# Row-wise cosine similarity on one core: hardware loops per engine with aligned heads, other pieces of the last two blocks, and stores awaited behind a manual section

## The chip, the cores and the metric

One core of a Trainium2 chip runs the whole program. The time is device microseconds (us) of one execution. The kernel before takes 1251.18 us (median of 4 runs in the comparison, 1250.94 to 1251.31). The profile is one execution recorded by the hardware profiler. Its span, from the first to the last instruction, is about 1.8 us shorter than the time of the same run.

## The reference

```python
x, y: 8192 x 8192, float32
x_norm = np.linalg.norm(x, axis=1, keepdims=True)
y_norm = np.linalg.norm(y, axis=1, keepdims=True)
return np.sum(x * y, axis=1) / (x_norm.squeeze() * y_norm.squeeze() + 1e-8)
```

Every element is read once: 536.87 MB. ACT squares and sums x and y, and DVE forms the dot product.

## The kernel before

The first 60 row blocks of 128 rows come in 30 groups of two blocks. Each group is one 8 MB load of x and one of y, so 60 loads go into three slots. The last four blocks are loaded in pieces that get smaller towards the end, so that little is left to compute when the last byte lands. A framework makes the waits between instructions. It unrolls everything: there is no branch between the first load and the end.

```python
PIECES = {
    nt - 4: [("x", 8192, "A"), ("y", 8192, "A")],
    nt - 3: [("x", 8192, "A"), ("y", 8192, "A")],
    nt - 2: [("x", 8192, "A"), ("y", 4096, "A"), ("y", 4096, "A")],
    nt - 1: [("x", 4096, "A"), ("y", 3072, "A"), ("x", 2432, "A"), ("y", 1792, "A"),
             ("y", 1408, "A"), ("x", 1024, "A"), ("y", 640, "A"), ("y", 640, "A"),
             ("x", 640, "V"), ("y", 256, "A"), ("y", 384, "A")],
}   # "A": ACT squares this piece, "V": DVE does
# ... cut: the slots, the sums, the first load ...
for g in range(G):                                     # G = 30, unrolled
    xt, yt = xs.pop(g), ys.pop(g)
    c = 2 * g
    cut = 2 * K - SIDE
    square(xt[:, 0:K], col(XX, c))                     # ACT
    square(xt[:, K:], col(XX, c + 1))
    # ... cut ...
    nc.vector.tensor_copy(out=side, in_=xt[:, cut:])   # DVE
    dot(xt[:, 0:K], yt[:, 0:K], col(XY, c), xt[:, 0:K])
    dot(xt[:, K:cut], yt[:, K:cut], part, xt[:, K:cut])
    square(yt[:, 0:K], col(YY, c))
    square(yt[:, K:], col(YY, c + 1))
    dot(side, yt[:, cut:], col(XY, c + 1), side, part)
    if g + 1 < G:
        load(g + 1)
# ... cut: for each piece of the last blocks a square and, for y, a dot ...
    if b == last - 1:
        finish(nt - NB, last)      # square root and reciprocal of the finished blocks
# ... cut: the last chain: base <- sums of the parts; last dot; transposes; product; store ...
```

Of the kernel before, what the change touches and what calls it, by code (L numbers as in the profile page):

```python
# [7 lines left out]


FP32 = mybir.dt.float32  # L10
U8 = mybir.dt.uint8
ALU = mybir.AluOpType
ACTF = mybir.ActivationFunctionType
AX = mybir.AxisListType
EPS = 1e-8
XX, YY, XY = 0, 1, 2


def lead_with_first_load(nc):


    blocks = nc.m.functions[0].blocks
    opening, body = blocks[0], blocks[1]
    load = next(i for i in body.instructions if i.opcode == "DMACopy")
    assert not load.sync_info.on_wait
    rest = [i for i in body.instructions if i.name != load.name]
    head = list(opening.instructions)
    at = next(n for n, i in enumerate(head) if i.opcode == "Drain" and i.engine == load.engine)
    head.insert(at, load)
    body.instructions = rest  # L30
    opening.instructions = head
# [3 lines left out]
def kernel(  # L35
# [6 lines left out]
    nc = tc.nc  # L42
    P = nc.NUM_PARTITIONS
    nc.at_finalize(lead_with_first_load)
    n_rows, K = x.shape
    nt = n_rows // P

# [3 lines left out]
    NB = 4  # L51
    G = (nt - NB) // 2
    SIDE = 4096
    BANK = 512
    VJUNK = 3072

    xg = x[0:G * 2 * P, :].rearrange("(g p j) k -> g p (j k)", p=P, j=2)
    yg = y[0:G * 2 * P, :].rearrange("(g p j) k -> g p (j k)", p=P, j=2)
# [4 lines left out]
    PIECES = {  # L63
        nt - 4: [("x", 8192, "A"), ("y", 8192, "A")],
        nt - 3: [("x", 8192, "A"), ("y", 8192, "A")],
        nt - 2: [("x", 8192, "A"), ("y", 4096, "A"), ("y", 4096, "A")],
        nt - 1: [("x", 4096, "A"), ("y", 3072, "A"), ("x", 2432, "A"), ("y", 1792, "A"),
                 ("y", 1408, "A"), ("x", 1024, "A"), ("y", 640, "A"), ("y", 640, "A"),
                 ("x", 640, "V"), ("y", 256, "A"), ("y", 384, "A")],
    }  # L70

    slots = ctx.enter_context(tc.tile_pool(name="slots", bufs=3))
    junkpool = ctx.enter_context(tc.tile_pool(name="junk", bufs=1))
    small = ctx.enter_context(tc.tile_pool(name="small", bufs=1))
    psumpool = ctx.enter_context(
        tc.tile_pool(name="psum", bufs=1, space=bass.MemoryType.PSUM))

    def slot(name):
        return slots.tile([P, 2 * K], FP32, tag="slot", name=name)

    xs, ys = {}, {}

    def load(g):
        xs[g] = slot(f"xg{g}")
        nc.sync.dma_start(out=xs[g], in_=xg[g])
        ys[g] = slot(f"yg{g}")
        nc.sync.dma_start(out=ys[g], in_=yg[g])

    def load_block(b):
        s = slot(f"b{b}")  # L90
        xs[b], ys[b] = s[:, 0:K], s[:, K:]
        at = {"x": 0, "y": 0}
        for which, w, _ in PIECES[b]:
            a = at[which]
            at[which] = a + w
            dst, src = (xs[b], xv) if which == "x" else (ys[b], yv)
            nc.sync.dma_start(out=dst[:, a:a + w], in_=src[b, :, a:a + w])

    load(0)

    sums = small.tile([P, 3, nt], FP32, tag="sums")
    norm = small.tile([P, 2, nt], FP32, tag="norm")
    den = small.tile([P, nt], FP32, tag="den")
    ident = small.tile([P, P], FP32, tag="ident")
    dummy = small.tile([P, 1], FP32, tag="dummy")
    junk = junkpool.tile([P, K], U8, tag="junk")
    vjunk = junkpool.tile([P, VJUNK], U8, tag="vjunk")

    nc.scalar.memzero(dummy)  # L109
    nc.scalar.sqrt(out=dummy, in_=dummy)  # L110
    make_identity(nc, ident)

    def square(src, acc, into=junk):
        nc.scalar.activation(out=into, in_=src, func=ACTF.Square, accum_out=acc)  # L114

    def dot(a, b, acc, into, init=0.0):
        nc.vector.tensor_tensor_reduce(  # L117
            out=into, in0=a, in1=b, scale=1.0, scalar=init, op0=ALU.mult, op1=ALU.add,
            accum_out=acc)

    def col(q, c):
        return sums[:, q, c:c + 1]
# [3 lines left out]
    for g in range(G):  # L126
        xt, yt = xs.pop(g), ys.pop(g)
        c = 2 * g
        cut = 2 * K - SIDE
        square(xt[:, 0:K], col(XX, c))  # L130
        square(xt[:, K:], col(XX, c + 1))
        side = psumpool.tile([P, SIDE], FP32, tag="side", name=f"side{g}")
        part = small.tile([P, 1], FP32, tag="part", name=f"part{g}")
        nc.vector.tensor_copy(out=side, in_=xt[:, cut:])  # L134
        dot(xt[:, 0:K], yt[:, 0:K], col(XY, c), xt[:, 0:K])
        dot(xt[:, K:cut], yt[:, K:cut], part, xt[:, K:cut])
        square(yt[:, 0:K], col(YY, c))
        square(yt[:, K:], col(YY, c + 1))
        dot(side, yt[:, cut:], col(XY, c + 1), side, part)
        if g + 1 < G:  # L140
            load(g + 1)

    for b in PIECES:
        load_block(b)

    def finish(a, b):

        c = slice(a, b)
        nc.scalar.activation(out=norm[:, :, c], in_=sums[:, 0:2, c], func=ACTF.Sqrt)  # L149
        nc.vector.tensor_mul(out=den[:, c], in0=norm[:, 0, c], in1=norm[:, 1, c])  # L150
        nc.vector.tensor_scalar_add(out=den[:, c], in0=den[:, c], scalar1=EPS)
        nc.vector.reciprocal(out=den[:, c], in_=den[:, c])  # L152

    def store_groups(ps):
        c = slice(0, 2 * G)
        res = small.tile([P, 2 * G], FP32, tag="res")
        nc.vector.tensor_mul(out=res, in0=sums[:, XY, c], in1=den[:, c])  # L157
        orow = small.tile([G, P, 2], FP32, tag="orow")
        for j in range(2):
            nc.tensor.transpose(out=ps[j], in_=res[:, j:2 * G:2], identity=ident)  # L160
            nc.vector.tensor_copy(out=orow[:, :, j], in_=ps[j])  # L161
        nc.sync.dma_start(
            out=out[0:G * 2 * P].rearrange("(g q) -> g q", q=2 * P),
            in_=orow.rearrange("g p j -> g (p j)"))


    tail = psumpool.tile([P, SIDE], FP32, tag="side", name="tail")
    pst = [tail[0:G, j * BANK:j * BANK + P] for j in range(2)]
    psl = [tail[0:NB, j * BANK:j * BANK + P] for j in range(2, 4)]


    ring = {"A": 0, "V": 0}

    def room(engine, w):
        tile_, size = (junk, K) if engine == "A" else (vjunk, VJUNK)
        a = ring[engine] if ring[engine] + w <= size else 0
        ring[engine] = a + w
        return tile_[:, a:a + w]

    last = nt - 1  # L180
    for b, pieces in PIECES.items():
        nx = sum(1 for q in pieces if q[0] == "x")
        ny = len(pieces) - nx
        parts = sums[:, :, b:b + 1]
        if ny > 1:
            m = max(nx, ny - 1 if b == last else ny)
            parts = small.tile([P, 3, m], FP32, tag=f"parts{b}", name=f"parts{b}")
            nc.vector.memzero(parts)
        if b == last:
            base = small.tile([P, 3], FP32, tag="base")  # L190
            fin = small.tile([P, 1], FP32, tag="fin")
        at, k = {"x": 0, "y": 0}, {"x": 0, "y": 0}
        for n, (which, w, engine) in enumerate(pieces):
            a, i = at[which], k[which]
            at[which], k[which] = a + w, i + 1
            src = (xs if which == "x" else ys)[b][:, a:a + w]
            if b < last or n < len(pieces) - 1:
                acc = parts[:, XX if which == "x" else YY, i:i + 1]
                xy, init = parts[:, XY, i:i + 1], 0.0
            else:  # L200
                nc.vector.tensor_reduce(out=base, in_=parts, axis=AX.X, op=ALU.add)  # L201
                acc, xy, init = fin, col(XY, last), base[:, XY:XY + 1]
            if engine == "A":
                square(src, acc, room("A", w))
            else:
                dot(src, src, acc, room("V", w))
            if which == "y":
                xp = xs[b][:, a:a + w]
                dot(xp, src, xy, room("V", w) if w <= VJUNK else xp, init)
        if ny > 1 and b != last:  # L210
            nc.vector.tensor_reduce(  # L211
                out=sums[:, :, b:b + 1], in_=parts, axis=AX.X, op=ALU.add)
        if b == nt - 4:
            finish(0, 2 * G)
            store_groups(pst)
        if b == last - 1:
            finish(nt - NB, last)

# [44 lines left out]
```

## Time and profile before

| | kernel before |
|---|---|
| time, median | 1251.18 us |
| first slot landed (ACT's first square starts at 21.98) | 21.95 us |
| 60th slot landed | 1165.48 us |
| last input landed | 1244.08 us |
| last dot starts | 1245.58 us |
| last store's receipt (the signal that it is complete) | 1248.63 us |
| span | 1249.46 us |

Landings are read from the semaphore increments of each load, of which the sixteenth counts (the trace of before has 1269 increments: 16 for each of the 78 loads and the first store, 5 for the last store); the small tables of this document use them. The profile's page gives the overview. Its DMA row shows the busy share of the DMA engines in tenths over 40 equal slices, and the next row the rate. The section of queues shows packets, megabytes and the share of time.

```profile
span 1249.5 us, 876 instructions
...
PE 1.3 (0%) x4; PEld 0.3 (0%) x4; DVE 700.5 (56%) x250; ACT 916.4 (73%) x283; POOL 0.7 (0%) x6
...
DMA  9999999999999999999999999999999999999997
GB/s 434 434 409 434 436 436 436 437 435 436 434 432 430 420 434 436 436 436 436 436 434 434 432 437 424 424 437 434 436 434 436 436 436 434 432 430 426 428 426 317
...
q1 hardware_dynamic: 11285, 536.91, 99.5%
q14 instruction: 7, 0.06, 0.0%
```

The stream of inputs bounds the kernel: DMA is busy at nine tenths in 39 of 40 slices while ACT is busy for 73% and DVE for 56%. The last line: seven packets of the queue that the profile names "instruction" (called instruction packets here), 0.06 MB against 537, or 0.0% of the time.

The timeline gives the places where time can still be won. Its columns are start, duration, engine, line, operation, output and input, and in brackets the idle time before and what ended it.

```profile
0.80 1.28 ACT L109 ACT_TABLE_LOAD   x1 [0.80 <-PEq L247]
...
21.98 7.03 ACT L114 ACTIVATE junk<-xg 128x8192 uint8<-128x8192 f32 x1 [18.16 <-DMA xg<-in_x_dram]
...
1165.56 7.03 ACT L114 ACTIVATE junk<-yg 128x8192 uint8<-128x8192 f32 x1 [5.08 <-DMA yg<-in_y_dram]
...
1228.70 0.19 ACT L114 ACTIVATION_READ_ACCUMULATOR junk<-b 128x1 f32 x1
...
1230.46 0.16 DVE L211 TENSOR_REDUCE sums<-parts 128x3 f32<-128x6 f32 x1
1230.66 0.21 ACT L149 ACTIVATE norm<-sums 128x6 f32<-128x6 f32 x1 [1.77 <-DVE sums L211]
1230.77 3.60 ACT L114 ACTIVATE junk<-b 128x4096 uint8<-128x4096 f32 x1
...
1245.24 0.51 ACT L114 ACTIVATE junk<-b 128x384 uint8<-128x384 f32 x1
1245.37 0.17 DVE L201 TENSOR_REDUCE base<-parts 128x3 f32<-128x18 f32 x1 [0.97 <-ACT junk L114]
1245.58 0.62 DVE L117 CUSTOM_DVE_ANT_0 vjunk<-b,base 128x384 uint8<-128x384 f32 x1
...
1247.46 0.27 SPq L232 DMA_DIRECT2D out_dram<-orl  x1
```

ACT waits 1.77 us for a reduction of DVE before the square root at 1230.66 and is late from there on. The last dot at 1245.58 starts 1.5 us after its data.

### The profile page before, as it was taken

The page shows a single profiled execution, that of the slowest core. Times are in us where ns is not written, and L with a number is a line of the kernel's source. Part 1 is how long each engine was busy: PE and PEld are TensorE (multiplying, and loading weights), DVE is VectorE, ACT ScalarE, POOL GpSimd, SP SyncE. Part 2 cuts the span into 40 slices and gives each one's busy share as a digit, 9 for nine tenths or more (in the row PEclk, how much of TensorE's full clock was granted, in tenths as well). Part 3 has the DMA queues.
Part 4 walks back from the last instruction along what each step waited for, and adds up shares of the span by engine and source line. Part 5 has one row for each costly group of instructions (what it writes and reads, how often), then busy time and mean ns, then how long its engine had stood idle before and what let it go on. Part 6 is the DMA issues. An engine that isn't in the chain of part 4 may idle for free.

```text
span 1249.5 us, 876 instructions
## 1 busy us (share of the span) xinstructions
PE 1.3 (0%) x4; PEld 0.3 (0%) x4; DVE 700.5 (56%) x250; ACT 916.4 (73%) x283; POOL 0.7 (0%) x6
## 2 busy tenths in 40 slices
PE   0000000000000000000000000000000000000000
PEld 0000000000000000000000000000000000000000
DVE  1654576544765446754467544675445755457566
ACT  3686776866867768677686776866867768677888
POOL 0000000000000000000000000000000000000000
DMA  9999999999999999999999999999999999999997
GB/s 434 434 409 434 436 436 436 437 435 436 434 432 430 420 434 436 436 436 436 436 434 434 432 437 424 424 437 434 436 434 436 436 436 434 432 430 426 428 426 317
DMA packets 11292, 536.97 MB, mean 430 GB/s; under 512 B 1267, under 2 KB 1557, under 8 KB 2325
## 3 DMA queue, kind: packets, MB, share of 16 engines
q1 hardware_dynamic: 11285, 536.91, 99.5%
q14 instruction: 7, 0.06, 0.0%
HBM read 536.87 MB, written 0.03 MB: 430 GB/s over the span
## 4 chain that ended last, share of the span: by engine, by line
DMA 65%; DVE 33%; ACT 1%; issue 1%; PE 0%; DVEq 0%; ACTq 0%; SPq 0%
DMA yg<-in_y_dram 63%; DVE xg L117 31%; DMA b<-in_x_dram 2%; ACT junk L114 1%; DVE b L117 1%; DVE side L117 0%; DVEq L117 0%; DVE vjunk L117 0%; DVE part L117 0%; PE tail L229 0%; PE tail L223 0%; DVE sums L117 0%; DVE orl L231 0%; DVE base L201 0%; DVE sums L211 0%
## 5 line engine op out<-in xcount | busy, mean ns | idle before, releaser
L117 DVE CUSTOM_DVE_ANT_0 xg<-xg,yg 128x8192 f32<-128x8192 f32 (+1 forms) x60 | 391.1, 6557 | 449.3 <-DMA yg<-in_y_dram 449.3
L114 ACT ACTIVATE junk<-xg 128x8192 uint8<-128x8192 f32 x60 | 421.8, 7029 | 167.5 <-DMA xg<-in_x_dram 166.6
L114 ACT ACTIVATE junk<-yg 128x8192 uint8<-128x8192 f32 x60 | 421.8, 7030 | 153.8 <-DMA yg<-in_y_dram 152.9
L134 DVE COPY side<-xg 128x4096 f32<-128x4096 f32 x30 | 132.8, 4428 | 71.2 <-DMA xg<-in_x_dram 71.2
L117 DVE CUSTOM_DVE_ANT_0 side<-side,yg,part 128x4096 f32<-128x4096 f32 x30 | 134.8, 4493 | 1.1
L114 ACT ACTIVATE junk<-b 128x8192 uint8<-128x8192 f32 (+9 forms) x17 | 57.3, 3373 | 6.0 <-DMA b<-in_x_dram 3.4
L117 DVE CUSTOM_DVE_ANT_0 b<-b 128x8192 f32<-128x8192 f32 (+1 forms) x4 | 26.1, 6552 | 14.7 <-ACT junk L114 8.4
L117 DVE CUSTOM_DVE_ANT_0 vjunk<-b 128x640 uint8<-128x640 f32 (+4 forms) x7 | 9.7, 1414 | 3.1 <-DMA b<-in_y_dram 3.0
L114 ACT ACTIVATION_READ_ACCUMULATOR junk<-yg 128x1 f32 x60 | 11.2, 186 | 0.0
L114 ACT ACTIVATION_READ_ACCUMULATOR junk<-xg 128x1 f32 x60 | 11.2, 186 | 0.0
L117 DVE DVE_READ_ACCUMULATOR2_ANT sums<- 128x1 f32 x63 | 7.0, 111 | 0.0
L114 ACT ACTIVATION_READ_ACCUMULATOR junk<-b 128x1 f32 x17 | 3.2, 187 | 0.0
L150 DVE TENSOR_TENSOR den<-norm 128x60 f32<-128x60 f32 (+1 forms) x2 | 0.4, 192 | 4.2 <-ACT norm L149 4.2
L117 DVE DVE_READ_ACCUMULATOR2_ANT part<- 128x1 f32 x30 | 2.5, 83 | 0.0
L109 ACT ACT_TABLE_LOAD x1 | 1.3, 1283 | 0.8 <-PEq L247 0.8
L160 PE MATMUL tail<-ident,res 128*30 128x128 f32 x2 | 0.6, 396 | 1188.6 <-DVE res L157 1188.6
L149 ACT ACTIVATE norm<-sums 128x120 f32<-128x120 f32 (+1 forms) x2 | 0.5, 247 | 1.8 <-DVE sums L211 1.8
L110 ACT ACT_TABLE_LOAD x1 | 1.3, 1283 | 0.0
L161 DVE COPY orow<-tail 30x128 f32<-30x128 f32 x2 | 0.5, 278 | 0.6 <-PE tail L160 0.6
L152 DVE RECIPROCAL den<-den 128x60 f32<-128x60 f32 (+1 forms) x2 | 0.7, 352 | 0.1
L117 DVE DVE_READ_ACCUMULATOR2_ANT parts<- 128x1 f32 x9 | 0.7, 82 | 0.0
L201 DVE TENSOR_REDUCE base<-parts 128x3 f32<-128x18 f32 x1 | 0.2, 172 | 1.0 <-ACT junk L114 1.0
(24 smaller groups left out, 5.2 us busy)
## 6 DMA issues: line engine op xcount, KB each, us to landing
b<-in_x_dram SPq DMA_DIRECT2D x3, 4096.0 KB, 30.6
b<-in_y_dram SPq DMA_DIRECT2D x2, 4096.0 KB, 39.9
b<-in_y_dram SPq DMA_DIRECT2D x2, 2048.0 KB, 37.7
b<-in_x_dram SPq DMA_DIRECT2D x1, 2048.0 KB, 30.6
b<-in_y_dram SPq DMA_DIRECT2D x1, 1536.0 KB, 33.9
b<-in_x_dram SPq DMA_DIRECT2D x1, 1216.0 KB, 36.4
b<-in_y_dram SPq DMA_DIRECT2D x1, 896.0 KB, 38.1
b<-in_y_dram SPq DMA_DIRECT2D x1, 704.0 KB
```

The source lines that it names most:

```text
L109: nc.scalar.memzero(dummy)
L110: nc.scalar.sqrt(out=dummy, in_=dummy)
L114: nc.scalar.activation(out=into, in_=src, func=ACTF.Square, accum_out=acc)
L117: nc.vector.tensor_tensor_reduce(out=into, in0=a, in1=b, scale=1.0, scalar=init, op0=ALU.mult, op1=ALU.add, accum_out=acc)
L134: nc.vector.tensor_copy(out=side, in_=xt[:, cut:])
L149: nc.scalar.activation(out=norm[:, :, c], in_=sums[:, 0:2, c], func=ACTF.Sqrt)
L150: nc.vector.tensor_mul(out=den[:, c], in0=norm[:, 0, c], in1=norm[:, 1, c])
L152: nc.vector.reciprocal(out=den[:, c], in_=den[:, c])
L160: nc.tensor.transpose(out=ps[j], in_=res[:, j:2 * G:2], identity=ident)
L161: nc.vector.tensor_copy(out=orow[:, :, j], in_=ps[j])
L201: nc.vector.tensor_reduce(out=base, in_=parts, axis=AX.X, op=ALU.add)
```

## The change

The intent is threefold. The 30 groups become hardware loops, one per engine, in a section whose waits are written by hand; the heads of ACT's and DVE's loops are put at a given slot of the code (`head_slot`, here 66, is the slot asked for; this is called alignment below). The last two blocks get other pieces, and the square root of the finished blocks moves behind five pieces of the last one. The waits for the two stores move behind the section. The diff, cut to its core:

```diff
-    load = next(i for i in body.instructions if i.opcode == "DMACopy")
-    ... (first load put ahead of the first Drain of its engine)
+    at = 1 + next(n for n, i in enumerate(head)
+                  if i.opcode == "ISA" and i.engine == load.engine)
+    closing = blocks[-1]
+    ... (every wait on a "stored" semaphore is moved to the head of the closing block)
 
-    for g in range(G):
-        ... (unrolled, waits by the framework)
+    with tc.tile_critical():
+        with nc.sync.Fori(0, R - 1) as r: ...                       # loads
+        with nc.tensor.Fori(0, R): ...                              # passes landings on
+        with nc.Fori(0, 1, engines=(ACT,), head_slot={ACT: 66}): ... # table loads
+        with nc.scalar.Fori(0, R) as r: ...                         # squares
+        with nc.Fori(0, R, engines=(DVE,), head_slot={DVE: 66}) as r: ... # dots
 
-        nt - 2: [("x", 8192, "A"), ("y", 4096, "A"), ("y", 4096, "A")],
-        nt - 1: [("x", 4096, "A"), ("y", 3072, "A"), ... 11 pieces, one "V"]
+        [("x", 8192, "A"), ("y", 4736, "A"), ("y", 3456, "A")],
+        [("x", 3968, "A"), ("y", 3200, "A"), ("x", 2176, "A"), ("y", 640, "V"),
+         ("y", 1024, "A"), ("y", 1280, "A"), ("x", 896, "A"), ("y", 896, "A"),
+         ("x", 768, "A"), ("y", 384, "A"), ("y", 384, "A"), ("x", 384, "V"),
+         ("y", 384, "A")],
 
-        if b == last - 1:
-            finish(nt - NB, last)
+                if b == last and n == 4:
+                    act.wait(m_sum)
+                    ... (the same square root and reciprocal)
     ... (cut: one semaphore per piece, the same last chain, the store)
```

## The prediction

> **What bounds the kernel now.** The input stream. The slice table shows DMA at nine tenths in 39 of 40 slices, mostly 434 to 437 GB/s; ACT is 73% busy, DVE 56%. In the timeline one 8 MB slot lands every 19.35 us; a 64 KB packet takes 2.42 us, and 512 per DMA engine make about 1239 us, which the change does not shorten. What is left is small: about 2.6 us before the first slot's steady stream, about 2 us by which 59 slot intervals exceed 19.35 us, and 5.4 us from the last landing (1244.1) to the end (1249.5).
>
> **In the stream.** Of the 2 us, the late slots include those landing at 254.8 (+0.16), 293.8 (+0.32), 739.2 (+0.27), 758.6 (+0.12) and 836.6 (+0.56). The packet records show an 8 KB instruction packet of 0.31 to 0.33 us in each of those intervals (queue section: 7 in all). The lateness, 1.4 us in sum, is never made up. [...] these five should go. [...] Before has no branch in the stream, so its trace can't show this. Gain: 1.4 us. Other loop overhead (waits, branches, addresses) falls in slack: each x load is issued about 21 us, each y load about 6 us, before the queue would run dry.
>
> **In the tail.** ACT is late. In the timeline it waits from 1228.9 to 1230.66 for the sums of the third of the last four blocks, because the square root of the finished blocks stands there in its order, though the last block's first piece landed at 1228.84. It then runs without a gap to 1245.75, so the last dot starts at 1245.58, 1.5 us after its data. The change moves that square root behind five pieces of the last block and gives DVE two squares (640 and 384 columns) instead of one. A replay with durations of the trace (ACT 0.19 + 0.833 us per 1000 columns, DVE 0.16 + 1.04) has ACT caught up by its fourth piece and the last dot starting 0.3 to 0.5 us after its landing. Gain 1.1 to 1.3 us. Two more pieces cost about 0.07 us each (a packet takes some 8.5 ns beyond its bytes, 8 per engine).
>
> **Neutral.** Own semaphores per piece remove waits of DMA issues on earlier landings (33 us in the queue's waits), but the queue is never dry there. The store's receipt (1.2 us) overlaps a section barrier, but two closing barriers (0.7 us) remain. The first load stands behind one instruction: 0 to 0.2 us lost. Extra waits in the last chain: about 0.1 us.
>
> **Sum.** 1251.26 - 1.4 - 1.2 + 0.15 + 0.2 = about 1249.0; with some chance that the unexplained lateness at 80 to 160 us (0.4 us) also goes, I predict 1248.8 us, range 1247.4 to 1250.6. Faster by over 2%: 0.01; within 2%: 0.97; slower by over 2%: 0.02.
>
> **What would show it.** Right: 0 to 2 instruction packets in the looped stretch, the 60th slot landing near 1164.1 instead of 1165.5, short gaps of ACT in the last 8 us, the last dot within 0.5 us of the last landing, that landing near 1242.8, the chain after it still about 3.9 us. Wrong: instruction packets every loop turn, DMA packets other than 64 KB, slot intervals above 19.35.
>
> **What would make it wrong.** [...] a late slot release by extra waits; a slower opening.

Three passages are cut where it is marked: two gave grounds for the loops and their heads to save instruction packets, one named a risk to the heads. No term of the sum goes with them: 1251.26 - 1.4 - 1.2 + 0.15 + 0.2 is 1249.01, and the chance of another 0.4 us makes it 1248.8. The 1.4 us of lateness is read from the trace of before. The 8.5 ns behind the 0.15 is an estimate: in before a packet of 1024 bytes takes 46 ns, where the rate of the 64 KB packets (2421 ns) gives 38. The 0.2 for the first load and the extra waits is the author's estimate (SP waits 0.2 us once at the opening of before), and no run tests it by itself.

## The result, and the profile after

The kernel after takes 1251.64 us (median of 4 runs, 1251.48 to 1251.67) against 1251.18 us before. The ratio is 1.0004 with a 95% interval of 0.9986 to 1.0021. A ratio is the mean time of one kernel's runs over that of the other's in the same rounds, so it is not quite the ratio of the medians quoted. The time did not fall by the 2.4 us predicted; it is outside the stated range of 1247.4 to 1250.6.

The page of the kernel after, the same lines:

```profile
span 1249.8 us, 1795 instructions
...
PE 1.3 (0%) x4; PEld 0.3 (0%) x4; DVE 698.2 (56%) x252; ACT 916.9 (73%) x285; POOL 0.8 (0%) x8
...
DMA  9999999999999999999999999999999999999997
GB/s 431 424 424 434 437 432 436 434 436 436 434 434 432 432 430 428 436 434 434 434 436 436 434 434 432 432 430 430 434 434 434 434 436 436 434 434 432 419 427 311
...
q1 hardware_dynamic: 11573, 536.91, 99.5%
q14 instruction: 7, 0.06, 0.0%
```

The instruction packets are still seven. Their times have moved. The DMA view cut to a window counts them: before has none up to 20 us, five from 20 to 1160 us and one from 1160 to 1245 us, as follows (two windows, in this order).

```profile
q14 instruction: 5, 0.04, 0.0%
...
q14 instruction: 1, 0.01, 0.0%
```

After, the windows are 0 to 20, 20 to 1160 and 1160 to 1245 us:

```profile
q14 instruction: 4, 0.03, 0.4%
...
q14 instruction: 1, 0.01, 0.0%
...
q14 instruction: 1, 0.01, 0.0%
```

The timeline after, at the places shown of before. The engines' waits are now instructions of their own, so the brackets name the sequencer (ACTq, DVEq) instead of the DMA:

```profile
8.14 1.28 ACT L202 ACT_TABLE_LOAD   x1 [8.14 <-issue]
...
24.02 7.03 ACT L143 ACTIVATE junk<-slot 128x8192 uint8<-128x8192 f32 x1 [12.79 <-ACTq L140]
...
1165.86 7.03 ACT L143 ACTIVATE junk<-slot 128x8192 uint8<-128x8192 f32 x1 [5.02 <-ACTq L140]
...
1239.25 0.19 ACT L343 ACTIVATE bnorm<-bsum 128x6 f32<-128x6 f32 x1
...
1245.04 0.18 DVE L314 TENSOR_REDUCE base<-parts 128x3 f32<-128x21 f32 x1
...
1245.36 0.62 DVE L146 CUSTOM_DVE_ANT_0 vjunk<-slot,base 128x384 uint8<-128x384 f32 x1
...
1247.12 0.29 SPq L398 DMA_DIRECT2D out_dram<-orl  x1
```

ACT's first table load starts at 8.14 us instead of 0.80, the first slot is taken up at 24.02 instead of 21.98, and yet the 60th is taken up within 0.3 us of before. It even landed 0.15 us earlier; ACT takes it up 0.53 us after its landing instead of 0.08. The news now comes by way of PE, but what the 0.45 us more consist of was not taken apart. The square root now waits for nothing. The balance of the two profiled runs, with what the prediction had for each term:

| term (us) | before | after | difference | predicted |
|---|---|---|---|---|
| start to 60th slot landed | 1165.48 | 1165.33 | -0.15 | -1.4 |
| 60th slot to last landing | 78.60 | 79.49 | +0.89 | +0.15 |
| last landing to last dot | 1.49 | 0.54 | -0.95 | -1.2 |
| last dot to receipt of the last store | 3.05 | 2.94 | -0.11 | +0.1 |
| receipt to end of the span | 0.83 | 1.53 | +0.70 | 0 |

So the question is not one but three: why the stream kept its length although the landings became regular, what lengthened the end of the stream, and what was added after the last receipt.

### Sixteen rings

Each 8 MB load is 128 packets of 64 KB and 16 of 4 bytes (9 ns each) in the trace, and the page counts 16 DMA engines. The trace's packet records don't name the engine, but following the end of a packet to the start of the next, mostly 3 or 4 ns before that end, separates the records into 16 chains of eight 64 KB packets per load. They are called rings here, and one ring is taken for all that one DMA engine carries, data and instructions. Up to the 60th slot all data packets but those of 4 bytes are of 64 KB and long, and the chains can be followed (where two end within nanoseconds of each other, they may be exchanged). In the end part of after the chains stay ambiguous, so nothing is read from them there except where one packet's neighbours are meant. Lateness is a ring's end of its 60th slot minus the same constant in every run: 21.40 us and 59 slots of 19.344 us, that is eight packets of 2.418 us each.

```
kernel   ring late (us)   instruction packets on that ring (us)
before   2.30             277.8, 820.5
before   1.77             239.1, 742.9          (and 1217.9)
before   1.08             756.7
before   0.25 to 0.92     none (13 rings)
after    2.14             6.7, 12.4             (and 1217.7)
after    1.98             6.6, 12.0, 126.4
after    -0.01 to 1.66    none (14 rings)
```

In these traces the packets of one sequencer come on one ring. In before, the packets of 239.1, 742.9 and 1217.9 us come at ACT's 62nd, 192nd and 320th instruction, those of 277.8 and 820.5 at DVE's 61st and 187th: one per 128 or so. A packet costs its ring more than its own 0.31 to 0.33 us, because the 64 KB packet behind it is longer too:

```
before, DVE's ring: start, duration (ns), bytes
275366   2418   65536
277780    321    8192     instruction packet
278089   3080   65536     2420 is usual
281166   2418   65536
```

Together that is 0.98 to 0.99 us for DVE's two packets in before, 0.63 and 0.70 for ACT's; the packets of the first 13 us cost 0.5 us or more. The lateness stays to the 60th slot, as the table shows. A slot counts as landed with its sixteenth increment, and that follows the slowest ring: its 60th slot ends at 1165.00 us in before and 1164.83 in after, the sixteenth increment comes 0.48 and 0.49 us later. That the slowest ring alone sets the landing is the theory to test, the slowest-ring theory. Its rivals are the sum theory of the prediction (each packet adds its own time to the stream, wherever it falls) and a natural-spread theory (rings drift some 2 us apart whatever is fetched).

### The profile page after: what moved, and what is told of

It is laid out like the page before. It is cut to its first block, busy times and chain, and to the rows that moved or that the text cites. A ratio compares the mean times of both kernels' runs of the same rounds, so it can differ in the third digit from the quotient of the medians.

```text
span 1249.8 us, 1795 instructions
## 1 busy us (share of the span) xinstructions
PE 1.3 (0%) x4; PEld 0.3 (0%) x4; DVE 698.2 (56%) x252; ACT 916.9 (73%) x285; POOL 0.8 (0%) x8
## 5 line engine op out<-in xcount | busy, mean ns | idle before, releaser
L143 ACT ACTIVATE junk<-slot 128x8192 uint8<-128x8192 f32 (+4 forms) x138 | 900.9, 6528 | 320.9 <-ACTq L140 314.7
L146 DVE CUSTOM_DVE_ANT_0 slot<-slot,slot 128x4096 f32<-128x4096 f32 (+1 forms) x60 | 391.1, 6557 | 452.4 <-DVEq L140 452.4
L222 DVE COPY side<-slot 128x4096 f32<-128x4096 f32 x30 | 132.8, 4428 | 72.9 <-DVEq L140 72.9
L146 DVE CUSTOM_DVE_ANT_0 side<-side,slot,part 128x4096 f32<-128x4096 f32 x30 | 134.7, 4490 | 0.0
L146 DVE CUSTOM_DVE_ANT_0 slot<-slot 128x8192 f32<-128x8192 f32 (+3 forms) x5 | 29.7, 5945 | 20.9 <-ACT junk L143 12.7
L143 ACT ACTIVATION_READ_ACCUMULATOR junk<-slot (+1 forms) x138 | 25.7, 186 | 0.0
L146 DVE CUSTOM_DVE_ANT_0 vjunk<-slot 128x384 uint8<-128x384 f32 (+4 forms) x8 | 6.8, 887 | 0.9 <-DMA slot<-in_y_dram 0.9
L146 DVE DVE_READ_ACCUMULATOR2_ANT gsum<- x60 | 6.8, 113 | 0.0
```

Source lines behind the costliest of these rows:

```text
L143: return nc.scalar.activation(out=into, in_=src, func=ACTF.Square, accum_out=acc)
L146: return nc.vector.tensor_tensor_reduce(out=into, in0=a, in1=b, scale=1.0, scalar=init, op0=ALU.mult, op1=ALU.add, accum_out=acc)
L222: nc.vector.tensor_copy(out=side, in_=xt[:, CUT:])
```

## The experiments

Each kernel was run in five rounds; the runs of the kernel before beside them have medians of 1251.17 to 1251.20 us. All results were correct. The first four ran on one chip, as did the next four and the last three. So experiments 6 and 9 to 11 are compared with experiment 2 across chips; the medians of before beside them differ by 0.03 us.

### 1. No alignment of the loop heads

```diff
-with nc.Fori(0, 1, engines=(ACT,), head_slot={ACT: 66}):
+with nc.Fori(0, 1, engines=(ACT,)):
-with nc.Fori(0, R, engines=(DVE,), head_slot={DVE: 66}) as r:
+with nc.Fori(0, R, engines=(DVE,)) as r:
```

> The kernel after without the two head alignments. Slowest-ring theory: each 8 KB instruction packet makes its one DMA ring 0.65 to 1.0 us late for good, all packets of ACT fall on one ring and all of DVE on another, and the slowest ring ends the stream. Then four packets of the first 13 us go, the first slot lands near 21.95 instead of 23.59, the 60th near 1164.2 instead of 1165.3, the last landing near 1243.1, and the time is about 1250.0 (1.6 under after). Natural-spread theory (the rings drift about 2 us apart whatever is fetched): the 60th slot still lands near 1165.3 and the time is 1251.6. If the unaligned loops refetch every turn: tens of instruction packets and 1255 or more.

Measured: 1249.93 us (1249.64 to 1250.18; before 1250.85 to 1251.52 over 9 runs, so no overlap; ratio 0.999, interval 0.9976 to 1.0003). The first slot lands at 21.84, the 60th at 1164.01, the last input at 1243.25. The page counts three instruction packets instead of seven, and the timeline has ACT's table load back at the start:

```profile
q14 instruction: 3, 0.02, 0.0%
```

```profile
1.06 1.28 ACT L202 ACT_TABLE_LOAD   x1 [1.06 <-SPq L168]
...
22.27 7.03 ACT L143 ACTIVATE junk<-slot 128x8192 uint8<-128x8192 f32 x1 [18.12 <-ACTq L140]
```

It follows that the four early packets of after come from the alignment alone. The loops without it bring no instruction packets per turn: one packet from 20 to 1160 us.

### 2. Heads at slot 80

```diff
-head_slot={ACT: 66} ... head_slot={DVE: 66}
+head_slot={ACT: 80} ... head_slot={DVE: 80}
```

> The kernel after with both loop heads at slot 80 instead of 66. [...] no packets at 6 to 13 us, and the same gain as without alignment (about 1250.0). If any alignment costs the jump: four early packets again and about 1251.6.

A guess at where the two slots lie in the code is cut, since no run looked at it; "the jump" is the branch into the aligned code shown below.

Measured: 1249.96 us (1249.55 to 1250.23), three instruction packets, none before 91.3 us. Alignment at slot 80 does no harm (1249.93 without alignment). The instruction records show a branch of ACT into the aligned code (line 201) at 1.05 us with either slot. Behind it the table load starts at 1.20 us with slot 80:

```profile
1.20 1.28 ACT L202 ACT_TABLE_LOAD   x1 [1.20 <-SPq L168]
```

With slot 66 it starts at 8.14 us, after the packet at 6.6 us: 7.1 us pass between the branch and the table load. In the same way 7.5 us pass on DVE, from its branch at 1.13 us (line 218) to its next instruction at 8.60. Why slot 66 brings the packets and slot 80 does not is not shown; where the loops are placed was not looked at.

### 3. More instructions on DVE, kernel before

```diff
+        for _ in range(9):
+            nc.vector.memzero(spare)          # 128 x 1, in each of the 30 groups
```

> The kernel before with nine tiny DVE memsets more in each of the 30 groups (270 instructions, two more 8 KB packets of DVE within the stream; some 20 us of DVE time where it idles 16 us per group). Slowest-ring theory: the two land on the ring that DVE's packets already slow (2.3 us late at the 60th slot), at 1.0 us each: 60th slot near 1167.4, time about +1.8. Sum theory of the prediction (each packet adds its own 0.31 us to the stream wherever it falls): +0.6. Natural-spread theory: +0.

Measured: 1253.07 us (1252.81 to 1253.19; ratio 1.0015, interval 1.0001 to 1.0029), +1.87 us. The framework moved many of the memsets to the start, so DVE's packets are at 11.6, 31.7, 221.4 and 783.5 us, four instead of two up to the 60th slot. Three of the landings behind them are 0.96 to 0.99 us late, and the 60th comes at 1167.17 (+1.70). The two extra packets cost 0.85 us each, nearly three times their own length, as the slowest-ring theory says. The sum theory (+0.6) and natural spread (0) are out.

### 4. More instructions on GpSimd, kernel before

```diff
     make_identity(nc, ident)
+    for _ in range(256):
+        nc.gpsimd.memset(spare, 0.0)
```

> The kernel before with 256 tiny GpSimd memsets at the start (two more 8 KB packets, of an engine that has none so far). Slowest-ring theory: they land on a ring of their own, which ends up 1.3 to 2.0 us late, not later than the slowest today (2.3): first slot 1.3 to 2 us late, 60th slot within 0.2 us of 1165.5, time +0 to +0.2. Sum theory: +0.6 or more. Natural-spread theory: +0.

Measured: 1250.97 us (1250.86 to 1251.37), -0.2 us. Two more packets, at 11.8 and 31.6 us, are there, on a ring of their own, which is 1.60 us late at the 60th slot; the first landing comes 0.46 us later than in before (1.3 to 2 were expected, but only one of the two packets comes ahead of it) and the 60th at 1165.59 (+0.11). The same number of extra packets as in experiment 3 costs nothing. This is the clearest separation of the theories: here it matters not how many packets there are but how many fall on the ring that is last.

### 5. Only the square root moved, kernel before

```diff
-        if b == last - 1:
-            finish(nt - NB, last)
+            if b == last and n == 4:
+                finish(nt - NB, last)
```

> The kernel before with only the square root of the finished blocks moved behind five pieces of the last block (pieces and all else as before). Stall theory of the prediction (that square root alone makes ACT late): the last dot starts about 0.3 to 0.5 us after its landing instead of 1.5, time -1.0. Shared theory (with the old pieces DVE becomes the late engine, since it has the four last dots and one square to do): the last dot still starts 1.0 to 1.2 us late, time -0.3 to -0.5; the new pieces are needed for the rest. Last landing unchanged near 1244.1.

Measured: 1251.21 us (1250.95 to 1251.83), no change. It tests nothing, as its timeline shows:

```profile
1230.33 0.16 DVE L213 TENSOR_REDUCE sums<-parts 128x3 f32<-128x6 f32 x1
1230.52 0.21 ACT L149 ACTIVATE norm<-sums 128x6 f32<-128x6 f32 x1 [1.77 <-DVE sums L213]
1230.64 3.60 ACT L114 ACTIVATE junk<-b 128x4096 uint8<-128x4096 f32 x1
```

The square root still stands ahead of the last block's first square, because the framework orders the instructions itself. The question went to experiment 11, in the manual section, where the order written is the order run.

### 6. Heads at slot 80 with the pieces of before

The edit puts the two lists of pieces of the kernel before into the version of experiment 2.

> The version with heads at slot 80, with the pieces of before. Two DMAs fewer: the last landing 0.15 us earlier. Stall theory: the last dot still about 0.5 us after it, time -0.1 against the new pieces (1249.85). Shared theory: the last dot 1.0 to 1.2 us after it, time +0.4 to +0.6 (1250.4).

Measured: 1249.95 us (1249.62 to 1250.49). The last dot starts 1.08 us after the last landing, against 0.55 with the new pieces: the shared theory holds for that term.

```profile
1244.10 0.62 DVE L145 CUSTOM_DVE_ANT_0 vjunk<-slot,base 128x384 uint8<-128x384 f32 x1
```

The time is the same all the same. The last landing was 0.07 us later in this profile, although two DMAs fewer were to bring it 0.15 us earlier, and from the receipt to the end it took 1.10 us against 1.53. That 0.43 us is another matter, see experiment 9.

### 7 and 8. One head aligned alone

The kernel after with the alignment at 66 of DVE's loop only, and of ACT's only.

> The kernel after with only DVE's loop head aligned at 66. Slowest-ring theory: DVE's ring keeps its three packets at 1.0 us (two of them in the first 13 us) and stays the slowest, so freeing ACT's ring gains nothing: first slot near 23.6, last landing near 1244.8, 1251.5. Sum theory: half of the gain of removing both, 1250.8.

> The kernel after with only ACT's loop head aligned at 66. Slowest-ring theory: ACT's ring has its three packets at about 0.68 us (2.0), DVE's only one (1.0), so the stream ends about 0.9 us earlier than in after: first slot near 22.8, last landing near 1243.9, 1250.7. Sum theory: 1250.8. Together with the run that aligns DVE alone: slowest ring wants 1251.5 and 1250.7, sum wants the same for both.

Measured: DVE alone 1251.66 us (1251.31 to 1251.83), ACT alone 1250.62 us (1250.46 to 1250.88). With DVE's the first slot lands at 23.72 and the last input at 1244.97; with ACT's at 22.92 and 1243.76. Both have five instruction packets in all. Removing the same number of packets gains nothing in one case and 1.0 us in the other, as the slowest-ring theory said in numbers (1251.5 and 1250.7). The traces show where the 1.0 us arises: the 60th slot still lands at the same time (1165.47 with DVE's, 1165.32 with ACT's, each with one ring of early packets), and from there to the last landing it takes 79.50 us against 78.44. In that part another packet of DVE's comes in both (1217.8 and 1205.9 us), and only with DVE's head aligned is its ring already the last.

### 9. Twelve instructions more on SP

In the runs with the manual section before this one, SP stands still near the end for about 0.36 us more than usual, mostly between two drains (instructions of the closing barriers). The instruction records of SP in the version of experiment 2 and in this one, from the receipt on (start in us, instruction):

```
heads at 80            1246.456 semaphore wait   1246.526 drain   1246.952 drain
with twelve more       1246.610 semaphore wait   1246.677 drain   1246.737 drain
```

```diff
+        pad = sem("pad")
+        for _ in range(12):
+            nc.sync.sem_inc(pad, 1)           # SP, between its loop and the last loads
```

> The version with heads at slot 80 and twelve semaphore increments more on SP, between its loop and the last loads, where SP has some 20 us to spare. In all runs with the manual section and the new pieces SP stands still for 0.36 us more between two drains after the last store's receipt; with the old pieces (two DMA issues fewer on SP) the same 0.36 us sat two drains later. Code-position theory: the stop belongs to a place in SP's code, so twelve more instructions move it ahead of the last DMA issue, where SP waits for 12 us anyway; receipt to end falls from 1.53 to about 1.15 and the time by about 0.4, to 1249.6. If it belongs to the drain or to the manual section itself: 1.53 and 1249.96 as before.

Measured: 1249.44 us (1249.26 to 1249.46; ratio 0.9985, interval 0.9971 to 0.9999). From the receipt to the end it takes 1.04 us instead of 1.53. The instruction packet that came at 1247.9 us, after SP's stop, comes at 1225.3 us. The stop is found ahead of the last loads: SP stands still from 1221.37 to 1221.79 us between two DMA issues, where it takes 0.05 us in experiment 2. In both it comes ahead of SP's 304th instruction in the trace, and so it does in every run with the manual section (in experiment 6 that is another drain, in experiment 10 the first drain). So the stop belongs to a place in SP's code. An instruction packet comes 1.0 us after the end of the stop in experiment 2 and 3.5 us after it here; that the two belong together is not shown. This version is the fastest that was run: 1.7 us under before and 2.2 under after, and the only one faster than before whose interval leaves out 1.

### 10. Store waits inside the section

The moving of the waits into the closing block is taken out of the version of experiment 2.

> The version with heads at slot 80 with the waits for the two stores left inside the manual section (that part of the change undone). The section's own barrier (about 0.45 us from its first instruction to SP's last in the trace) then follows the receipt instead of overlapping it: time +0.4 to +0.5 against the waits behind the section (1250.4), unless SP's 0.36 us stop moves too.

Measured: 1250.52 us (1250.22 to 1250.79), +0.56 against the waits behind the section. From receipt to end it takes 2.10 us instead of 1.53. The move does what it was meant to do, but the section that needs it came with the change. Before has neither, and needs 0.83.

### 11. The square root early, in the manual section

```diff
-                if b == last and n == 4:
+            if b == last - 1:
                     act.wait(m_sum)
```

> The version with heads at slot 80 and new pieces, with the square root of the finished blocks put back ahead of the last block (now in the order that the program gives, since the manual section is not rescheduled). Stall theory: ACT waits about 1.5 us for the sums of the block before, never catches up, and the last dot starts about 1.5 us after its landing instead of 0.55: time +0.9 to +1.1 (1250.9 to 1251.1). If the pieces alone do it: no change.

Measured: 1250.55 us (1250.44 to 1250.76), +0.59 against experiment 2. The last dot is 1.27 us late instead of 0.55. Its timeline:

```profile
1229.30 0.16 DVE L342 TENSOR_REDUCE bsum<-parts 128x3 f32<-128x6 f32 x1
1229.50 0.21 ACT L347 ACTIVATE bnorm<-bsum 128x6 f32<-128x6 f32 x1 [1.85 <-DVE bsum L342]
...
1244.07 0.17 DVE L314 TENSOR_REDUCE base<-parts 128x3 f32<-128x21 f32 x1 [0.71 <-ACT junk L143]
1244.39 0.62 DVE L146 CUSTOM_DVE_ANT_0 vjunk<-slot,base 128x384 uint8<-128x384 f32 x1
```

ACT stops for 1.85 us, and at the end DVE waits 0.71 us for ACT's last square but one. Both parts are needed: the early square root costs 0.72 us of lateness with the new pieces, and the old pieces cost 0.53 with the late square root. I had expected +0.9 to +1.1 and overrated it: ACT makes up some of its lateness with the new pieces.

## Why the prediction was wrong

**The bound was right.** The stream bounds the kernel in both traces, at 19.35 us per slot; nothing in the loops slowed it.

**The step that failed first: "these five should go", "Gain: 1.4 us".** Two things are wrong with it. First, the packets in the loop went, but four others came in their place. The stretch from 20 to 1160 us has one packet instead of five, as the prediction's own mark of 0 to 2 had it; but four are now in the first 13 us, put there by the alignment at slot 66 (experiments 1 and 2), and they make the first slot 1.64 us late (23.59 against 21.95). A slower opening was listed among the risks, without a size or a cause. What the traces show of the cause is the entry into the loop: with slot 66 ACT branches at 1.05 us, a packet comes at 6.6 us and the table load behind the branch starts at 8.14; with slot 80 no packet comes before 91.3 us, and the table load behind the same branch starts at 1.20. The prediction's grounds for expecting the loops and the aligned heads to save packets were shown by no trace, and are cut.

Second, the delays were put down to the stream as a whole, as if one pipe had suffered all five. Successive landings show only the growth of the slowest ring. By ring, DVE's ring had two packets at about 1.0 us and ended 2.30 us late, and it has two and ends 2.14 us late in after. The landings became regular in after because all the lateness is there from the first slot on; the total is almost the same. One of the five is misread besides: the slot of 739.2 landed on time (738.79) and ACT took it up late; both packets, at 742.9 and 756.7 us, fall into the next interval, which is 0.40 us too long. These faults did not spoil the size. With these packets gone but for one (experiments 1 and 2) the 60th slot lands at 1164.01 and 1163.87, and the prediction's mark of 1164.1 is met. The size was about right for a kernel without these packets, and the change was not that kernel.

**The end of the stream: +0.89 measured, +0.15 predicted.** Two DMAs more were counted, DVE's third packet was not. It comes after DVE's loop, at 1217.7 us, on the ring that is already last. ACT's packet at 1217.9 us in before fell on the ring that was second. In before, DVE's third packet (by its count of instructions) comes at 1246.8 us, after the data. The trace of after shows the cost: the instruction packet takes 333 ns, and the packet of 18944 bytes behind it 1367 ns where about 709 are usual, 0.99 us in sum. The version with DVE's head alone aligned keeps the whole loss and the one with ACT's alone gives up 1.0 us of it (experiments 7 and 8), which agrees. The two DMAs more cost nothing that can be seen: with heads at slot 80 the part from the 60th slot to the last landing takes 79.11 us with the old pieces and 79.10 with the new.

**The tail of computation: right mechanism, gain 0.95 instead of 1.2.** The last dot starts 0.54 us after its landing, where "within 0.5" was said. Both the moved square root and the new pieces are needed (experiments 6 and 11).

**"Two closing barriers (0.7 us) remain" as neutral: wrong by 0.70 us.** From receipt to end it is 1.53 us instead of 0.83. About 0.49 of that is SP's stop, which experiment 9 removed. The clearing of the semaphores takes 0.268 us instead of 0.096; that this is so because more of them are in use was not tested, and the rest was not taken apart.

**Sum.** The predicted -2.4 us was made of -1.4, -1.2 and small losses. Measured are -0.15 + 0.89 - 0.95 - 0.11 + 0.70 = +0.38 us in the span (0.37 before rounding), and +0.46 between the medians.

**Open.** Why a 64 KB packet behind an instruction packet takes 0.2 to 0.66 us more, and why it is more for DVE's packets than for ACT's, was not tested. Some rings without instruction packets are late as well (up to 1.66 us in after); they decide the landings ahead of the first instruction packet (in before 0.4 us of lateness up to 157.8 us), but not that of the 60th slot in the traces in which the rings were followed. What SP waits for in its 0.36 us is not shown.

## What to carry to other kernels

In a kernel at the limit of its DMA, count events per ring and take the maximum: in these runs a delay of one of 16 rings lasted to the 60th slot at least (2.30 us in before), two packets more on the ring that was last added up (1.70 us at the 60th slot in experiment 3), and two on another ring did not (0.11 us in experiment 4). An event that vanishes from the steady state may have moved to the first or last microseconds, so compare the first landing as well as the intervals. Where an alignment or a loop is meant to save instruction packets, count the instruction packets in the profile's queue section: a head at slot 66 instead of 80 cost four packets and 1.7 us here, and the position of twelve harmless instructions was worth 0.5 us.
